# ConvFFN products in another order on VectorE and GpSimd, and the last normalisation and its stores regrouped

## The chip, the cores and the metric

The kernel runs on one core of a Trainium2 chip. The metric is the device time of one execution in microseconds (us), as the median of several runs. Five engines matter. TensorE (PE in the profile, PEld for its weight loads) multiplies matrices into PSUM. [...] ScalarE (ACT) evaluates activation functions and copies. SyncE (SP) issues most of the DMA transfers; ACT's queue issues a few. Each engine executes its own list of instructions strictly in the order of that list; an instruction that waits holds up all that stand behind it on its engine.

## What is computed

One inference step of a decoder with two layers, for 256 prompt tokens and 8 sample tokens that go through together as 264 columns. Each layer has a mixer (attention beside a gating or pooling branch) and then a ConvFFN; a last RMSNorm gives `y`. The change touches the ConvFFN and the last RMSNorm:

```python
def rmsnorm(x, g):
    xf = x.astype(jnp.float32)
    y = xf * lax.rsqrt(jnp.mean(xf * xf, axis=-1, keepdims=True) + EPS)
    return (y * g).astype(x.dtype)

def conv_ffn(x, prev, norm_g, w_gate, w_up, conv_w, conv_b, w_down):
    T = x.shape[1]
    h = rmsnorm(x, norm_g)
    g = h @ w_gate
    g_all = jnp.concatenate([prev, g], axis=1)
    gc = sum(conv_w[i] * g_all[:, i:i + T] for i in range(CONV_W)) + conv_b
    a = jax.nn.gelu(gc) * (h @ w_up)
    return x + a @ w_down, g_all[:, -(CONV_W - 1):]
```

The model width is 1024, the FFN width 2816; all values are float32.

## The kernel before

**Layout.** Activations lie transposed: 128 partitions of one feature tile, 264 tokens along the free axis. The model width is 8 tiles (`KD`), the FFN width 22 tiles (`NF`). Each weight matrix is cut into blocks of 128x128, laid out in HBM in the order in which TensorE uses them.

**Precision by halves.** Every operand is split in a rounded high half and the remainder, the low half. A weight tile of eight blocks is read as `raw` by DMA, copied to `wh` on ACT (L311) and its remainder `wl` formed on DVE (L312), both from rings of four buffers: tile t+4 can be split only when TensorE is done with tile t. Each block then takes three matmuls (L334 high x high, L335 high weight x low activation, L336 low weight x high activation). Activations are split the same way, by `halves` (L418 on ACT, L419 on DVE) or by `operand_tile` (L378 on ACT, L379 on DVE).

**The ConvFFN.** `ffn(l, ...)` runs the blocks of 22 gate tiles and 22 up tiles in turn, g0 u0 g1 u1 g2 u2 and so on, eight blocks each; only the first four output tiles are interleaved by half their depth. The results accumulate in four PSUM banks (tag `mm`), so a fifth output tile needs a bank that an earlier one has left. For the first five tiles (`JN`) the operand is `xg`, the residual times the norm's gain without the norm's scale R per token; R is multiplied in afterwards. For the later tiles the operand is `xn`, normalised beforehand: `normalise(m)` multiplies the residual by R on GpSimd (L533, result `xr`, two buffers) and splits the product (L378, L379). Eight of these are placed by hooks between the blocks 40 and 68 of the FFN; the sixth gate tile, g5, is the first that needs them.

A gate tile's evacuation `evac` for j < 5 multiplies the bank by R into the buffer G (L543, DVE), then forms the convolution in C from G: L546 on ACT, L547, L548, L549 on DVE, and L550 on ACT copies the last columns of G out. L551 on ACT is the gelu. C and G are the two halves of one tile `wk`. An up tile's evacuation multiplies C by R on GpSimd (L557), then the up tile's bank by C on DVE into A (L558), and splits A into `a_h` and `a_l`. A lies where G lay.

**The end.** After the second FFN's down projection each of the 8 residual tiles gets its square (L391), its gain (L580), and GpSimd adds the squares up (L403). `finish` sums over partitions on TensorE (L411) and makes R (L413, L414). Then each tile of X is multiplied by R, tiles 2 and 5 on GpSimd and six on DVE (L1000), and five stores of 1, 1, 2, 2 and 2 tiles send X to `y`, in turn from SP's and ACT's queue (L1002).

**What sets the order.** The program is written in one order, but a planner arranges each engine's list at compile time by its own timeline of the program (`schedule_with_timeline_sim=True`); what is marked `keep_in_program_order` stays in place. So the list of an engine can change where its instructions' dependences change.

## Time and profile before

| quantity | value |
|---|---|
| median of 3 runs | 633.56 us (632.65 to 635.03) |
| the profiled execution's own time | 632.96 us |
| span of its profile | 630.9 us |
| TensorE busy | 611.6 us, 97% of the span |
| VectorE busy | 413.2 us, 65% |
| ScalarE busy | 343.8 us, 54% |
| GpSimd busy | 82.5 us, 13% |
| granted TensorE clock, mean | 0.994 |

The span goes from the first to the last instruction; the time of the execution holds some 2.1 us more than it. A row of the timeline has the start, the duration in us, the engine, the line, the operation, the output and inputs with their shapes, and in brackets the engine's idle time before it and what ended it. Instructions of one engine overlap a little: 0.43 us of a VectorE product with a start 0.34 us behind the one before is usual. A matmul of 264 columns is listed with 0.28 us, but one starts every 0.12 us. The table of stretches gives, for each, the busy time and the count of each engine's instructions, the granted clock (1.00 is full speed), the mean busy share of the core's 16 DMA engines, and the GB/s that they moved.

### The profile page before, as it was taken

How to read it: one execution, taken by the hardware profiler on the slowest of the kernel's cores; microseconds unless marked ns; L12 is line 12 of the kernel's file. 1: busy time of each engine (PE TensorE's matmuls, PEld its weight loads, DVE VectorE, ACT ScalarE, POOL GpSimd, SP SyncE). 2: the span in 40 equal slices, each digit the busy share in tenths (PEclk: the TensorE clock that was granted, in tenths of full speed). 3: DMA queues.
4: the chain of work that ended last, by engine and by line, in shares of the span. 5: the costliest groups of instructions: out<-in, count | busy, mean ns of one | idle time of the engine just before them, and what ended most of it. 6: DMA issues, size and time to landing. Idle time of an engine off the chain costs nothing.

```text
span 630.9 us, 12406 instructions
## 1 busy us (share of the span) xinstructions
PE 611.6 (97%) x4956; PEld 583.2 (92%) x4956; DVE 413.2 (65%) x690; ACT 343.8 (54%) x608; POOL 82.5 (13%) x111
## 2 busy tenths in 40 slices
PE   7899999998999999999999999999899999999994
PEld 5887997998999999999998886999899999999994
DVE  6895674959966676655654674396996667664442
ACT  6448653667665555644442664366766555564441
POOL 3320132324000000010110000032400000001021
PEclk8999999999999999999999999999999999999998
DMA  7995673543555455795477679354355545554501
GB/s 271 324 414 223 238 262 72 182 156 132 200 201 180 161 195 198 228 382 202 179 189 300 230 117 112 129 172 169 128 200 200 179 166 191 201 165 177 200 1 70
DMA packets 40971, 121.42 MB, mean 192 GB/s; under 512 B 17490, under 2 KB 18642, under 8 KB 29522
## 3 DMA queue, kind: packets, MB, share of 16 engines
q1 hardware_dynamic: 40050, 119.15, 57.2%
q10 hardware_dynamic: 864, 1.49, 0.7%
q8 instruction: 39, 0.64, 0.4%
q14 instruction: 18, 0.15, 0.1%
HBM read 116.68 MB, written 3.94 MB: 191 GB/s over the span
## 4 chain that ended last, share of the span: by engine, by line
PE 90%; DVE 4%; ACT 2%; DMA 2%; issue 1%; POOL 1%; SPq 0%; DVEq 0%; ACTq 0%; POOLq 0%
PE mm L334 27%; PE mm L335 27%; PE mm L336 26%; DMA raw<-in_w 2%; DVE wl L312 1%; PE pv_l L470 1%; PE sc L456 1%; ACT wh L311 1%; PE Z L880 1%; PE Z L868 1%; PE pav L499 1%; DVE xn_l L379 1%; PE S L655 1%; PE S L654 1%; PE po_l L483 1%
## 5 line engine op out<-in xcount | busy, mean ns | idle before, releaser
L312 DVE TENSOR_TENSOR wl<-raw,wh 128x1024 fp32r<-128x1024 f32 x183 | 229.1, 1253 | 135.1 <-ACT wh L311 135.1
L311 ACT ACTIVATE wh<-raw 128x1024 fp32r<-128x1024 f32 x183 | 193.4, 1059 | 204.9 <-PE mm L335 187.6
L335 PE MATMUL mm<-xn_l,wh 128*128 128x264 f32 x544 | 154.4, 284 | 0.0
L336 PE MATMUL mm<-xn_h,wl 128*128 128x264 f32 x544 | 154.1, 283 | 0.0
L334 PE MATMUL mm<-xn_h,wh 128*128 128x264 f32 x544 | 153.9, 283 | 0.0
L334 PEld LDWEIGHTS mm<-xn_h,wh 128*128 128x128 f32 x544 | 102.3, 188 | 0.0
L335 PEld LDWEIGHTS mm<-xn_l,wh 128*128 128x128 f32 x544 | 102.3, 188 | 0.0
L336 PEld LDWEIGHTS mm<-xn_h,wl 128*128 128x128 f32 x544 | 102.2, 188 | 0.0
L335 PE MATMUL mm<-a_l,wh 128*128 128x264 f32 x352 | 99.9, 284 | 0.0
L336 PE MATMUL mm<-a_h,wl 128*128 128x264 f32 x352 | 99.7, 283 | 0.0
L334 PE MATMUL mm<-a_h,wh 128*128 128x264 f32 x352 | 99.5, 284 | 0.0
L335 PEld LDWEIGHTS mm<-a_l,wh 128*128 128x128 f32 x352 | 66.2, 188 | 0.0
L336 PEld LDWEIGHTS mm<-a_h,wl 128*128 128x128 f32 x352 | 66.2, 188 | 0.0
L334 PEld LDWEIGHTS mm<-a_h,wh 128*128 128x128 f32 x352 | 66.1, 188 | 0.0
L334 PE MATMUL mm<-xg_h,wh 128*128 128x264 f32 x160 | 46.9, 300 | 4.2 <-ACT wh L311 2.5
L334 PE MATMUL mm<-xg_f_h,wh 128*128 128x264 f32 x160 | 46.2, 289 | 4.5 <-DVE wk L558 4.3
L335 PE MATMUL mm<-xg_l,wh 128*128 128x264 f32 x160 | 45.6, 291 | 0.0
L336 PE MATMUL mm<-xg_f_h,wl 128*128 128x264 f32 x160 | 45.3, 283 | 0.0
L335 PE MATMUL mm<-xg_f_l,wh 128*128 128x264 f32 x160 | 45.3, 283 | 0.0
L336 PE MATMUL mm<-xg_h,wl 128*128 128x264 f32 x160 | 45.2, 294 | 0.1
L334 PE MATMUL mm<-xg_n_h,wh 128*128 128x264 f32 x128 | 37.9, 296 | 0.0
L335 PE MATMUL mm<-xg_n_l,wh 128*128 128x264 f32 x128 | 37.0, 289 | 0.0
(257 smaller groups left out, 1088.5 us busy)
## 6 DMA issues: line engine op xcount, KB each, us to landing
raw<-in_w SPq DMA_DIRECT2D x89, 1024.0 KB, 4.8
K<-in_kt SPq DMA_DIRECT2D x32, 256.0 KB, 6.2
V<-in_vp SPq DMA_DIRECT2D x32, 256.0 KB, 5.4
raw<-in_w SPq DMA_DIRECT2D x5, 512.0 KB, 5.1
CST<-in_cst SPq DMA_DIRECT2D x1, 560.0 KB, 4.7
XG<-in_x ACTq DMA_DIRECT2D x1, 528.0 KB, 7.7
out_k<-k SPq DMA_DIRECT2D x1, 528.0 KB, 8.7
out_v<-v SPq DMA_DIRECT2D x1, 528.0 KB, 3.0
```

The lines of the kernel that those rows point to most:

```text
L311: s.activation(h, src, AF.Copy)
L312: v.tensor_tensor(l, src, h.bitcast(F32), ALU.subtract)
L334: pe.matmul(o, h[:, c:c + P], xh, start=first, stop=False)
L335: pe.matmul(o, h[:, c:c + P], xl, start=False, stop=False)
L336: pe.matmul(o, l[:, c:c + P], xh, start=False, stop=left[m] == 0)
L379: j = v.scalar_tensor_tensor(l, src, gain, h.bitcast(F32), ALU.mult, ALU.subtract)
L456: pe.matmul(ps[32 * t:32 * t + 32, :PAST].rearrange("p (g k) -> p g k", g=NPG), qz[:, t, sq, :], kt[sq][:, :, t * P:(t + 1) * P], start=sq ...
L470: pe.matmul(pv[32 * j:32 * j + 32, :], pz[:, pg, sq, :], vtiles[sq][:, pg, :], start=pg == 0, stop=pg == NPG - 1)
L483: pe.matmul(po[:, t * NS:(t + 1) * NS], msk[:, gr, 2 * t:2 * t + 2, :].rearrange("p h d -> p (h d)"), cst("selS")[:, gr * NS:(gr + 1) * NS ...
L499: pe.matmul(o, vt[:, 0, h * HD:(h + 1) * HD], w[:, :SEQ], start=True, stop=False)
L654: pe.matmul(ps[:, 0:P], qh[:, 0:P], kh[:, 0:P], start=True, stop=False, skip_group_check=True)
L655: pe.matmul(ps[:, P:384], qh[:, P:SEQ], kh[:, 0:SEQ], start=False, stop=False, skip_group_check=True)
```

## The change

In the first five tiles of each FFN the up tile's evacuation multiplies the bank by R on VectorE into A, and GpSimd then multiplies A by C in place. Before, GpSimd multiplied C by R, and VectorE then the bank by C. The number of operations and their shapes stay. At the end, all eight tiles of X are multiplied on VectorE, in five instructions of 1, 2, 2, 2 and 1 tiles with R broadcast over the tiles, each followed by its store; and `y` in HBM has the tile as its outermost axis, so that a store writes rows of 264 floats where a store of two tiles had written rows of 528. The host's transposition of the output follows.

```diff
-YG = (2, 5)
-YD = ((0, 1), (1, 2), (2, 4), (4, 6), (6, 8))
-YQ = 1
+YD = ((0, 1), (1, 3), (3, 5), (5, 7), (7, 8))
...
-    ("y", (P, KD, T)), ("k0", (P, 4, T)), ("v0", (P, 4, T)), ("bvn", (P, 4, NS)),
+    ("y", (KD, P, T)), ("k0", (P, 4, T)), ("v0", (P, 4, T)), ("bvn", (P, 4, NS)),
...
                 C, A = wk[:, 0, :], wk[:, 1, :]
                 if j < JN:
-                    g.tensor_tensor(C, C, R, ALU.mult)
-                v.tensor_tensor(A, o, C, ALU.mult)
+                    v.tensor_tensor(A, o, R, ALU.mult)
+                    g.tensor_tensor(A, A, C, ALU.mult)
+                else:
+                    v.tensor_tensor(A, o, C, ALU.mult)
                 halves(*hl(act, j), A)
...
     R = nrm.finish()
-    for m in range(KD):
-        (g if m in YG else v).tensor_tensor(X[:, m, :], X[:, m, :], R, ALU.mult)
     for i, (m, e) in enumerate(YD):
-        (s if YQ and i % 2 else nc.sync).dma_start(a["y"][:, m:e, :], X[:, m:e, :])
+        x = X[:, m:e, :]
+        v.tensor_tensor(x, x, R.unsqueeze(1).to_broadcast([P, e - m, T]), ALU.mult)
+        (s if i % 2 else nc.sync).dma_start(a["y"][m:e].rearrange("m p t -> p m t"), x)
```

More of the change, by code (lines that the diff above doesn't have):

```diff
@@ L1047 @@
     o = {n: np.asarray(r.results[0]["out_" + n]) for n, _ in _OUTS}
-    y = o["y"].transpose(2, 1, 0).reshape(T, D)
+    y = o["y"].transpose(2, 0, 1).reshape(T, D)
     def kv(k, w):
```

## The prediction

> **What bounds the kernel now.** I read the page first. TensorE is busy for 97% of the span, so what is not matmul time can only be had where TensorE stands still, and at the end, where it has nothing left to do. The list of who waited for whom, taken over the start of each FFN, names one such wait, for L558, the line that the change rewrites. TensorE's timeline gives its places, here the last matmul before each stop and the first one behind it:

> ```profile
> 140.91 0.28 PE L336 MATMUL mm<-xg_f_h,wl 128*128 128x264 f32 x1
> 141.75 0.36 PE L334 MATMUL mm<-xg_f_h,wh 128*128 128x264 f32 x1 [0.56 <-DVE wk L558]
> 150.41 0.28 PE L336 MATMUL mm<-xg_f_h,wl 128*128 128x264 f32 x1
> 150.81 0.36 PE L334 MATMUL mm<-xg_f_h,wh 128*128 128x264 f32 x1
> 153.65 0.28 PE L336 MATMUL mm<-xg_f_h,wl 128*128 128x264 f32 x1
> 155.55 0.36 PE L334 MATMUL mm<-xg_f_h,wh 128*128 128x264 f32 x1 [1.62 <-DVE wk L558]
> ...
> 453.65 0.28 PE L336 MATMUL mm<-xg_f_h,wl 128*128 128x264 f32 x1
> 455.49 0.36 PE L334 MATMUL mm<-xg_f_h,wh 128*128 128x264 f32 x1 [1.55 <-DVE wk L558]
> ```

> With 0.12 us from start to start as the usual pace, TensorE loses 0.72, 0.28 and 1.78 us, together 2.8 us, and the second FFN shows the same stops (1.72 us in the longest). That is the ceiling of what the first part of the change can give: about 2.8 us a layer, 5.5 us in both.

> The two long stops have different causes, as the chain of waits (start, duration, what) shows:

> ```profile
> 139.17 0.42 ACT wk L551
> ...
> 139.66 1.49 POOL wk L557
> ...
> 141.17 0.44 DVE wk L558
> ...
> 145.90 1.76 DVE wl L312
> ...
> 148.93 0.47 DVE wk L548
> ...
> 150.66 0.76 DVE wk L548
> 151.42 1.70 DVE wl L312
> 153.12 0.93 DVE xn_l L379
> ...
> 154.99 0.43 DVE wk L558
> ```

> At 141 the up tile u0 holds its bank until the gelu (L551) and GpSimd's product (L557) are done. At 155 the chain has run along VectorE alone since 145.90: u1's product stood in a full list. VectorE's stretches say the same (us; then busy time and count of PE, PEld, DVE, ACT, POOL; clock, DMA share, GB/s):

> ```profile
> 150.00:156.00 6.00, 4.27 (x34) 3.90 (x33) 6.00 (x10) 3.84 (x8) 4.42 (x6) 1.00 0.29 120
> 156.00:162.00 6.00, 6.00 (x52) 6.00 (x51) 6.00 (x11) 3.80 (x8) 1.41 (x2) 1.00 0.47 164
> ```

> From 150 to 162 VectorE never rests. And what ends this crowded stretch is the next thing that TensorE waits for: the last low half `xn_l`, without which g5 cannot finish.

> ```profile
> 161.09 0.48 DVE L379 SCALAR_TENSOR_TENSOR xn_l<-xr,VEC,xn_h 128x264 fp32r<-128x264 f32 x1
> 161.08 0.40 PE L334 MATMUL mm<-xn_h,wh 128*128 128x264 f32 x2
> 161.32 0.29 PE L335 MATMUL mm<-xn_l,wh 128*128 128x264 f32 x1
> ```

> TensorE arrives there with almost no slack (a step of 0.24 in place of 0.12 us). So two paths meet at 161.3: TensorE's with 2.8 us of stops, and VectorE's with hardly any. Taking the stops away helps only as far as VectorE's list gets shorter too.

> **The change part by part. First, the products of the FFN.** Five VectorE products and five GpSimd products per layer are exchanged for as many of the same shapes (bank times SBUF operand, SBUF times SBUF), so busy time stays: 0.43 us each on VectorE, up to 1.49 us on GpSimd. What moves is when the bank is left. The new product needs the up tile, R, and the buffer A, which is G's: it must come behind L548 and L550, the last readers of G.

> ```profile
> 137.84 0.47 DVE L548 SCALAR_TENSOR_TENSOR wk<-wk,VEC 128x254 f32<-128x254 f32 x1
> 139.30 1.23 DVE L312 TENSOR_TENSOR wl<-raw,wh 128x1024 fp32r<-128x1024 f32 x1 [0.99 <-ACT wh L311]
> 141.17 0.43 DVE L558 TENSOR_TENSOR wk<-mm,wk 128x264 f32<-128x264 f32 x1 [0.64 <-POOL wk L557]
> 142.20 1.23 DVE L312 TENSOR_TENSOR wl<-raw,wh 128x1024 fp32r<-128x1024 f32 x1 [0.60 <-ACT wh L311]
> 143.34 0.43 DVE L419 TENSOR_TENSOR a_l<-wk,a_h 128x264 fp32r<-128x264 f32 x1
> 143.68 0.77 DVE L543 TENSOR_TENSOR wk<-mm,R_f 128x264 f32<-128x264 f32 x2
> 145.90 1.76 DVE L312 TENSOR_TENSOR wl<-raw,wh 128x1024 fp32r<-128x1024 f32 x1 [0.65 <-ACT wh L311]
> ```

> For u0 that is 138.31 us, in an idle stretch of 0.99 us; its bank is free at 138.7 and the stop of 0.72 goes. For u1, L548 runs at 148.93 (chain), its bank is free by 149.8, before g4 asks for one at 150.5 (the 0.28 us). u2's follows behind the L548 that the chain has at 150.66, free by 151.9, before u4 asks at 153.8 (the 1.78 us). All three stops lose their cause.

> What is late next is `xn_l`. Between 142.20 and 161.57 VectorE works 18.7 us and idles 0.65. The list does not shrink; it can only start earlier. The chain of the first tile loses a link: GpSimd ends at 141.15 as before, and ScalarE can form `a_h` at once (0.41 us) in place of a VectorE product first, so L419 and the two L543 behind it (0.35 us each by their starts) can run from 141.6, in the 0.60 us that VectorE idles before the split at 142.20. The 0.65 us before 145.90 goes too, since that split waits through ScalarE for u2, which ends 0.72 us earlier. That is 1.25 us; against it, u3's product, now behind `xn_l` at 161.50, moves ahead of it and costs 0.35 us. Net 0.9 us, with the 0.12 us at 161.32 about 1.0 us a layer, 2.0 us in both. Bounds: -0.35 us a layer if the planner keeps the idle places, +2.8 us if it puts two splits of `a` and g4's product (0.35 us each) and one weight split (1.2 us) behind the last `xn_l`. I take the value between, for the rows show no slack of 2.8 us in VectorE's list but show 1.25 us.

> New waits: ScalarE's `a_h` now waits for GpSimd, and behind it stand weight copies L311. If it is put ahead of the one that now starts at 141.11, that copy is late by 0.4 us; the `wl` from it, ready at 143.4, is first used from 150.81, so this costs nothing, and without that cover it would cost 0.4 us. GpSimd's new product waits for the gelu as the old one did, with the same L533 behind it. VectorE waits for GpSimd only through `a_l`, where it had waited in L558.

> **Second, the end.** Rows of VectorE, GpSimd and the queues:

> ```profile
> 624.50 1.86 DVE L1000 TENSOR_TENSOR XG<-XG,R_fin 128x264 f32<-128x264 f32 x2
> 624.20 1.87 POOL L1000 TENSOR_TENSOR XG<-XG,R_fin 128x264 f32<-128x264 f32 x2 [8.93 <-ACT R_fin L414]
> 626.97 0.42 DVE L1000 TENSOR_TENSOR XG<-XG,R_fin 128x264 f32<-128x264 f32 x1
> 624.61 0.34 SPq L1002 DMA_DIRECT2D out_y<-XG  x1
> L309 DVE TENSOR_TENSOR wl<-raw,wh 128x512 fp32r<-128x512 f32 x1 | 0.7, 692 | 0.0
> L757 DVE TENSOR_TENSOR bv<-bv,mu 128x1056 f32<-128x1056 f32 x1 | 1.3, 1259 | 0.2 <-ACT mu L756 0.2
> 625.00:625.50 0.50, 0.00 (x0) 0.00 (x0) 0.50 (x2) 0.00 (x0) 0.50 (x2) 1.00 0.05 17
> 625.50:626.00 0.50, 0.00 (x0) 0.00 (x0) 0.50 (x1) 0.00 (x0) 0.50 (x1) 1.00 0.73 254
> 628.00:628.50 0.50, 0.00 (x0) 0.00 (x0) 0.00 (x0) 0.00 (x0) 0.00 (x0) 0.50 1.00 380
> 629.00:629.50 0.50, 0.00 (x0) 0.00 (x0) 0.00 (x0) 0.00 (x0) 0.00 (x0) 0.50 0.84 325
> ```

> Beside GpSimd's two products, until 626.07, two of VectorE's take 1.86 us together, where two such products take 0.77 us (the L543 above). Without GpSimd, five instructions follow from 624.15: one of 264 columns, three of 528 (0.71 us by the 692 ns for 512; the broadcast adds nothing, by the 1259 ns for 1056), one of 264. With an overlap of 0.08 us they end at 624.58, 625.21, 625.84, 626.47 and 626.82; the last product ended at 627.39. So VectorE is 0.57 us sooner.

> The DMA engines are full from 628 (share 1.00) to about 629.4 us (0.84 of the last half microsecond), so the end is set by bytes as well. The first store, issued at 624.61, shows data from about 625.47 (the share of 0.05 in 625.0 to 625.5), 0.86 us later. The second then starts at 626.09 and the rest follows without a gap: seven tiles of 135 KB, 946 KB. Rows of 1056 bytes moved at 254 GB/s with a share of 0.73, so 348 GB/s at a full share; rows of 2112 bytes at 380. All rows of `y` are now of 1056 bytes: 2.72 us at 348, end at 628.8; 2.47 us at about 383, end at 628.6. Against 629.4 this saves 0.6 to 0.85 us; I take 0.7. The bounds: 0 if the doubled number of rows costs as much as the earlier start gives (285 GB/s), 0.9 at best. The store's issue is 0.33 us on either queue, and behind these issues nothing stands.

> [...]

> **The sum.** 632.96 us for the profiled execution (630.9 of it span), less 2.0 and 0.7: 630.3. The profiled execution lies 0.6 us under the median of the runs, 633.56; on that scale the forecast is 630.9 us.

> **The rivals.** (B) VectorE's list makes full room: all stops go, 5.5 + 0.7 = 6.2 us, 627.4. For it: four or five instructions ahead of the last `xn_l` are not needed by TensorE soon. Against: the full rows from 150 to 162. (C) The FFN gains nothing, because the order is kept and `xn_l` stays at 161.5, or because the product queues behind L548 so long that the bank comes no earlier; the end alone gives 0.7: 632.9. For it: TensorE meets `xn_l` without slack now. Against: 1.25 us of idle VectorE time whose cause the change removes. (D) Slower: with the first tiles' gate products done earlier, the planner puts the convolutions of g1 and g2 and the new products (0.40 + 0.08 + 0.40 + 0.35 us by their starts, 1.23 us a tile) ahead of the first `xn_l`. The eight `normalise` steps pass through two buffers, GpSimd to ScalarE to VectorE, so a first one that is 2.46 us late makes the last one as late: TensorE waits in g5 until about 163.8, 2.4 us a layer, less 0.7 at the end: 637.7. It decides from the point where the last `xn_l` ends later than 161.57. For it: this is the order in which the program is written. Against: now `xn_l` comes first there.

> **How the numbers follow.** Chances: my forecast (A) 0.47, with its own range 629.3 to 632.3; B 0.22, C 0.22, D 0.09. The range reaches from B less a little scatter to C with the runs' scatter of about 1 us: 627.0 to 634.0; D lies outside. A measurement of this kernel can tell about 0.5%, 3.2 us, from no change: faster means under 630.4. That takes B whole and two fifths of A: 0.41. Slower, over 636.7, takes D: 0.08. The rest, 0.51, is the same.

> **What would show it.** In the changed profile: no TensorE stop that ends with an up tile's product; that product right behind L548 of its tile; the stop of g5 at `xn_l` grown to 1 to 2 us, with the last `xn_l` about 1 us earlier. A g5 without a stop means B; an `xn_l` after 161.6 means D. At the end, VectorE's last product near 626.8 on the old scale, less what the FFNs gave, and DMA engines full from 626.1 for 2.5 to 2.7 us. The forecast is wrong if stops for banks remain, or if the stores take longer than 3.3 us from there.

## The result, and the profile after

| | before | changed |
|---|---|---|
| median of 7 runs | 633.56 us (632.65 to 635.03) | 629.24 us (628.98 to 631.10) |
| ratio, with its 95% interval | 1 | 0.9936 (0.9921 to 0.9952) |
| profiled execution, its own time | 632.96 us | 629.23 us |
| its span | 630.93 us | 626.98 us |
| mean granted clock | 0.994 | 0.997 |

The changed kernel is 0.64% faster, 4.3 us by the medians and 3.95 us by the two spans. To see where it came from, the span is cut at four landmarks that both timelines have: ScalarE's copy of the 27th weight tile split there, which lies a little ahead of the first FFN, and the last residual sum of the first FFN, of the second mixer and of the second FFN (L575). Timelines of ScalarE (ACT in the rows) and VectorE (DVE), before and then changed (start, duration, engine, line, operation, tiles and shapes, and in brackets the idle time before it with what ended it):

```profile
114.50 1.06 ACT L311 ACTIVATE wh<-raw 128x1024 fp32r<-128x1024 f32 x1 [0.40 <-PE mm L335]
321.63 0.43 DVE L575 TENSOR_TENSOR XG<-XG,mm 128x264 f32<-128x264 f32 x1 [0.67 <-PE mm L336]
426.30 0.42 DVE L575 TENSOR_TENSOR XG<-XG,mm 128x264 f32<-128x264 f32 x1
621.44 0.43 DVE L575 TENSOR_TENSOR XG<-XG,mm 128x264 f32<-128x264 f32 x1 [7.59 <-PE mm L336]
```

```profile
114.15 1.06 ACT L309 ACTIVATE wh<-raw 128x1024 fp32r<-128x1024 f32 x1 [0.40 <-PE mm L333]
319.84 0.43 DVE L575 TENSOR_TENSOR XG<-XG,mm 128x264 f32<-128x264 f32 x1 [0.68 <-PE mm L334]
424.52 0.42 DVE L575 TENSOR_TENSOR XG<-XG,mm 128x264 f32<-128x264 f32 x1
617.99 0.43 DVE L575 TENSOR_TENSOR XG<-XG,mm 128x264 f32<-128x264 f32 x1 [7.59 <-PE mm L334]
```

Differences of these starts give the stretches (the last one runs to the end of the span): start 114.50 and 114.15, first FFN 207.13 and 205.69, second mixer 104.67 and 104.68, second FFN 195.14 and 193.47, end 9.49 and 8.99 us. So the first FFN gave 1.43 us, the second 1.66, the end 0.50 (differences from unrounded starts), the mixer nothing. The 0.35 us of the start belong to an execution, not to the change: that stretch comes out up to 2.3 us later in other kernels that share its code (last section).

In the changed kernel (line numbers two lower: matmuls L332 to L334, `xn_l` L377, the gate tile's last convolution step L546; the new products are L555 on VectorE and L556 on GpSimd, POOL in the rows) the list of who waited for whom at the start of the first FFN has one row for TensorE's matmuls, and TensorE's timeline shows its place (the second here) and a shorter stop ahead of it:

```profile
PE mm L333 <- DVE xn_l L377: 0.7, 1, 0.7
```

```profile
157.36 0.28 PE L332 MATMUL mm<-xn_h,wh 128*128 128x264 f32 x1
157.75 0.39 PE L333 MATMUL mm<-xn_l,wh 128*128 128x264 f32 x1
...
159.45 0.28 PE L333 MATMUL mm<-xn_l,wh 128*128 128x264 f32 x1
160.46 0.39 PE L333 MATMUL mm<-xn_l,wh 128*128 128x264 f32 x1 [0.73 <-DVE xn_l L377]
```

No stop ends with an up tile's product any more. The 0.72, 0.28 and 1.78 us of before are gone, and two stops for the last two `xn_l` have come: 0.27 and 0.89 us over the usual step. 2.78 us less 1.16 us is 1.62 us; the first FFN became 1.43 us shorter, so this account holds to 0.2 us. Counted matmul by matmul, the changed kernel is 1.65 us ahead from there to the end of the up tiles and loses the 0.2 us evenly over the down projection, without a stop; the second FFN (1.66 us) shows no such loss. VectorE's timeline shows what the stops now wait for:

```profile
137.49 0.48 DVE L546 SCALAR_TENSOR_TENSOR wk<-wk,VEC 128x254 f32<-128x254 f32 x1
138.00 0.43 DVE L555 TENSOR_TENSOR wk<-mm,R_f 128x264 f32<-128x264 f32 x1
...
141.28 0.43 DVE L417 TENSOR_TENSOR a_l<-wk,a_h 128x264 fp32r<-128x264 f32 x1 [1.11 <-ACT a_h L416]
141.63 0.77 DVE L541 TENSOR_TENSOR wk<-mm,R_f 128x264 f32<-128x264 f32 x2
...
148.61 0.42 DVE L555 TENSOR_TENSOR wk<-mm,R_f 128x264 f32<-128x264 f32 x1
...
150.07 0.42 DVE L555 TENSOR_TENSOR wk<-mm,R_f 128x264 f32<-128x264 f32 x1
...
157.96 0.42 DVE L555 TENSOR_TENSOR wk<-mm,R_f 128x264 f32<-128x264 f32 x1
158.30 1.21 DVE L310 TENSOR_TENSOR wl<-raw,wh 128x1024 fp32r<-128x1024 f32 x1
159.43 0.97 DVE L377 SCALAR_TENSOR_TENSOR xn_l<-xr,VEC,xn_h 128x264 fp32r<-128x264 f32 x1
```

The first up tile's product stands right behind L546 of its tile, the next two are done by 149.0 and 150.5. The split `a_l` (L417) runs at 141.28 where it ran at 143.34. From there on VectorE has no idle time at all, and the last `xn_l` ends at 160.40: 46.25 us behind the landmark, 47.07 before (161.57 less 114.50).

At the end, VectorE's five products and the stretches in which the stores move (columns: stretch, length, then busy time and count of PE, PEld, DVE, ACT, POOL; clock, DMA share, GB/s):

```profile
620.71 2.63 DVE L1001 TENSOR_TENSOR XG<-XG,R_fin 128x264 f32<-128x264 f32 x5 [2.29 <-ACT R_fin L412]
```

```profile
623.00:623.50 0.50, 0.00 (x0) 0.00 (x0) 0.34 (x1) 0.00 (x0) 0.00 (x0) 0.99 1.03 338
623.50:624.00 0.50, 0.00 (x0) 0.00 (x0) 0.00 (x0) 0.00 (x0) 0.00 (x0) 0.50 1.02 344
624.00:624.50 0.50, 0.00 (x0) 0.00 (x0) 0.00 (x0) 0.00 (x0) 0.00 (x0) 0.50 1.02 361
625.00:625.50 0.50, 0.00 (x0) 0.00 (x0) 0.00 (x0) 0.00 (x0) 0.00 (x0) 0.50 0.86 300
```

The products take 2.63 us where they took some 3.2 (624.15 to 627.39). The DMA engines are full from 623.0 to about 625.4, at 338 to 361 GB/s.

### The profile page after: what moved, and what is told of

It is laid out like the page before. It is cut to its first block, busy times and chain, and to the rows that moved or that the text cites. A ratio compares the mean times of both kernels' runs of the same rounds, so it can differ in the third digit from the quotient of the medians.

```text
span 627.0 us, 12404 instructions
## 1 busy us (share of the span) xinstructions
PE 610.4 (97%) x4956; PEld 581.9 (93%) x4956; DVE 414.2 (66%) x689; ACT 344.8 (55%) x608; POOL 84.0 (13%) x109
## 4 chain that ended last, share of the span: by engine, by line
PE 88%; DVE 6%; ACT 2%; issue 2%; DMA 1%; POOL 1%; SPq 0%; DVEq 0%; ACTq 0%; POOLq 0%
PE mm L332 26%; PE mm L333 26%; PE mm L334 26%; DVE wl L310 2%; DVE xn_l L377 1%; PE pv_l L468 1%; DMA raw<-in_w 1%; PE sc L454 1%; PE Z L880 1%; PE Z L868 1%; ACT wh L309 1%; PE pav L497 1%; DVE wk L545 1%; PE S L655 1%; PE S L654 1%
## 5 line engine op out<-in xcount | busy, mean ns | idle before, releaser
L309 ACT ACTIVATE wh<-raw 128x1024 fp32r<-128x1024 f32 x183 | 193.7, 1059 | 198.6 <-PE mm L333 184.9
L332 PE MATMUL mm<-xn_h,wh 128*128 128x264 f32 x544 | 153.9, 283 | 0.0
L334 PE MATMUL mm<-xn_h,wl 128*128 128x264 f32 x544 | 153.8, 283 | 0.0
L332 PEld LDWEIGHTS mm<-xn_h,wh 128*128 128x128 f32 x544 | 102.3, 188 | 0.0
L334 PEld LDWEIGHTS mm<-xn_h,wl 128*128 128x128 f32 x544 | 102.1, 188 | 0.0
L332 PE MATMUL mm<-a_h,wh 128*128 128x264 f32 x352 | 99.6, 284 | 0.0
L334 PE MATMUL mm<-a_h,wl 128*128 128x264 f32 x352 | 99.5, 283 | 0.0
L334 PEld LDWEIGHTS mm<-a_h,wl 128*128 128x128 f32 x352 | 66.2, 188 | 0.0
L332 PEld LDWEIGHTS mm<-a_h,wh 128*128 128x128 f32 x352 | 66.1, 188 | 0.0
L332 PE MATMUL mm<-xg_h,wh 128*128 128x264 f32 x160 | 46.4, 297 | 3.6 <-ACT wh L309 1.4
L334 PE MATMUL mm<-xg_h,wl 128*128 128x264 f32 x160 | 44.5, 290 | 1.3 <-DVE wl L310 1.3
L332 PE MATMUL mm<-xg_f_h,wh 128*128 128x264 f32 x160 | 45.7, 286 | 0.0
L334 PE MATMUL mm<-xg_f_h,wl 128*128 128x264 f32 x160 | 45.4, 283 | 0.0
L333 PE MATMUL mm<-xg_f_l,wh 128*128 128x264 f32 x160 | 45.3, 283 | 0.0
L332 PE MATMUL mm<-xg_n_h,wh 128*128 128x264 f32 x128 | 37.9, 296 | 0.0
```

Source lines behind the costliest of these rows:

```text
L309: s.activation(h, src, AF.Copy)
L332: pe.matmul(o, h[:, c:c + P], xh, start=first, stop=False)
L333: pe.matmul(o, h[:, c:c + P], xl, start=False, stop=False)
L334: pe.matmul(o, l[:, c:c + P], xh, start=False, stop=left[m] == 0)
```

## The experiments

Twelve kernels ran. The first table has their times beside the kernel before on the same chip; the second cuts their profiles into the stretches above, as differences from before, with TensorE's stops (over 0.15 us beyond the usual step) added up over each FFN stretch. The stretches are the finer instrument: the second mixer's reproduces to 0.01 us in all kernels but two (six tiles -0.20, fifth bank -0.08).

| kernel | runs | median us | before us | ratio (95%) |
|---|---|---|---|---|
| FFN products alone | 6 | 631.11 | 633.21 | 0.9963 (0.9945 to 0.9981) |
| end alone | 10 | 632.38 | 633.21 | 0.9989 (0.9975 to 1.0003) |
| changed, `y` in long rows | 6 | 629.84 | 633.21 | 0.9946 (0.9928 to 0.9965) |
| changed, A times C on VectorE | 5 | 628.58 | 633.21 | 0.9931 (0.9909 to 0.9954) |
| changed, six tiles | 4 | 628.15 | 632.81 | 0.9918 (0.9887 to 0.9949) |
| changed, four `xr` buffers | 6 | 629.50 | 632.81 | 0.9943 (0.9924 to 0.9963) |
| changed, `normalise` earlier | 4 | 629.02 | 632.81 | 0.9922 (0.9897 to 0.9948) |
| before, fifth bank | 10 | 631.01 | 632.81 | 0.9965 (0.9946 to 0.9983) |
| before, own banks for up tiles | 4 | 639.96 | 633.29 | 1.0109 (1.0088 to 1.0130) |
| all three, new products | 4 | 629.02 | 633.29 | 0.9932 (0.9914 to 0.9949) |
| all three, old products | 4 | 629.53 | 633.29 | 0.9936 (0.9914 to 0.9958) |
| all three, A times C on VectorE | 10 | 633.13 | 633.29 | 0.9996 (0.9976 to 1.0016) |

| profile | start | FFN 1 | FFN 2 | end | stops FFN 1, 2 |
|---|---|---|---|---|---|
| before (us) | 114.50 | 207.13 | 195.14 | 9.49 | 2.97, 2.90 |
| changed | -0.35 | -1.43 | -1.66 | -0.50 | 1.35, 1.30 |
| FFN products alone | +1.31 | -1.43 | -1.68 | +0.32 | as changed |
| end alone | -0.10 | +0.01 | +0.01 | -0.50 | as before |
| long rows | +2.34 | -1.44 | -1.66 | -0.85 | as changed |
| A times C on VectorE | +0.14 | -2.06 | -2.02 | -0.49 | 0.99, 0.98 |
| six tiles | +0.05 | -2.13 | -2.06 | -0.14 | 0.49, 0.66 |
| four `xr` buffers | -0.31 | -1.55 | -1.79 | -0.05 | 1.39, 1.35 |
| `normalise` earlier | +1.48 | -1.42 | -1.33 | -0.50 | 1.16, 1.15 |
| fifth bank | +4.11 | -2.84 | -3.19 | 0.00 | 0.98, 0.99 |
| own banks | +0.04 | +3.35 | +3.37 | 0.00 | 4.83, 4.82 |
| all three, new products | +1.57 | -1.57 | -1.49 | -0.40 | 1.59, 1.61 |
| all three, old products | +1.94 | -1.81 | -1.71 | -0.85 | 1.36, 1.38 |
| all three, A times C on VectorE | +0.63 | +0.50 | +0.58 | -0.85 | 2.13, 2.14 |

**The two parts alone.** The kernel before with only the five lines of the FFN products changed, and with only the end changed.

> The kernel before with the FFN products alone in the new order; end and stores as before. My theory (the banks of the up tiles are free earlier, and what is then late is the last low half xn_l on VectorE): the profile of the whole change shows 1.65 us gained in each FFN, so this kernel gains 3.3 us, span 627.6, time about 630.2 us. The longest wait of TensorE is about 0.9 us for xn_l in the sixth gate tile. Rival (the gain comes mostly from the end of the kernel): gain under 1 us, over 632.5 us.

> The kernel before with the end alone changed: products on VectorE by pairs, stores with the tile outermost; the FFN as before. My theory (the end is worth what its profile shows between the last residual sum and the end of the span, 0.5 us): span about 630.4, time 633.0 us. The rival above: over 3 us gained, about 630 us. The TensorE stops before the up tiles' banks stay, 0.72 and 1.78 us.

The FFN products alone give -1.43 and -1.68 us in the FFN stretches, what the whole change gives there; the end alone gives -0.50 us and leaves the FFNs as they were. The parts add up and don't touch each other. (The end stretch has scatter of its own: 9.49 us in three profiles with the old end and 9.81 in this one; with the new end 8.99 to 9.01 in four, 9.36 and 9.45 in two; with long rows 8.64 in three and 9.09 in one. The lower values are compared.) In whole times the first is 2.1 us (ratio below 1 with its interval), where 3.3 were expected: its profile has the gain in the FFNs, but a start 1.31 us and an end 0.32 us longer. The second is 0.8 us, with an interval that holds 1.

**Long rows of `y`.** The changed kernel, with `y` laid out as before, so that a store of two tiles writes rows of 2112 bytes:

```diff
-        (...).dma_start(a["y"][m:e].rearrange("m p t -> p m t"), x)
+        (...).dma_start(a["y"][:, m:e, :], x)
```

> The changed kernel with y in the layout of before, so that a store of two tiles writes rows of 2112 bytes; the products by pairs on VectorE stay. If the length of the rows sets the pace of the stores, the stretch with busy DMA engines at the end is shorter by 0.2 to 0.25 us (380 against 350 GB/s for 946 KB) and the kernel takes about 629.0 us. Rival (rows of 1056 bytes cost nothing, the stores wait for their issue): no difference in the end, 629.2 us, the same GB/s at a full share.

The end takes 8.64 us: the short rows cost 0.35 us. Its stores, in the same columns:

```profile
626.00:626.50 0.50, 0.00 (x0) 0.00 (x0) 0.02 (x1) 0.00 (x0) 0.00 (x0) 0.50 1.06 401
```

401 GB/s at a share of 1.06, against 338 to 361 at 1.02 to 1.03. Its whole time doesn't show the gain (0.9946 beside 0.9936); its profiled execution began 2.34 us late.

**A times C on VectorE.** The changed kernel with both products on VectorE, so that its list has five instructions more per layer:

```diff
-                    g.tensor_tensor(A, A, C, ALU.mult)
+                    v.tensor_tensor(A, A, C, ALU.mult)
```

> The changed kernel with the second product, A times C, on VectorE in place of GpSimd: five more VectorE instructions of 0.43 us a layer. If VectorE's full list sets the time of the last xn_l (my theory), the three of them that stand ahead of it make it 1.05 us later, the stop in g5 grows by that much, and the kernel loses about 2 us: 631.3 us. Rival (the latency of the chain through GpSimd sets it): the chain is 1.1 us shorter, the stop shrinks, and the kernel takes 628 us or less.

If the number of VectorE's instructions set the last `xn_l`, this would be slower. The FFN stretches became 0.63 and 0.36 us shorter still, so the expectation failed. The stop for `xn_l` is gone: the last one ends 0.67 us sooner, and the matmul that waits for it stands five places later in TensorE's list. Two short stops for a bank have come. The first waits for a gate product L541 that stands behind a weight split and `a_l` again (143.83 us, where the changed kernel has it at 141.63); the second comes while u1's product, which frees a bank at 148.61 us in the changed kernel, stands at 152.41. TensorE's and VectorE's timelines:

```profile
144.40 0.36 PE L332 MATMUL mm<-xg_f_h,wh 128*128 128x264 f32 x1 [0.17 <-DVE wk L541]
...
150.74 0.36 PE L332 MATMUL mm<-xg_f_h,wh 128*128 128x264 f32 x1 [0.30 <-DVE wk L541]
```

```profile
159.75 0.48 DVE L377 SCALAR_TENSOR_TENSOR xn_l<-xr,VEC,xn_h 128x264 fp32r<-128x264 f32 x1
```

The last `xn_l` takes 0.48 us here and 0.97 in the changed kernel, where GpSimd's new product runs beside it:

```profile
158.60 1.51 POOL L556 TENSOR_TENSOR wk<-wk 128x264 f32<-128x264 f32 x1 [1.19 <-DVE wk L555]
```

Both lose: the same GpSimd shape takes 0.75 us in other rows (`xr` at 150.39 in the changed kernel). The stretch of 148 to 162 us, in which VectorE never rests in either kernel, has the effect as a whole, changed and then this one:

```profile
148.00:162.00 14.00, 13.17 (x106) 12.75 (x105) 14.00 (x24) 9.53 (x18) 7.40 (x7) 1.00 0.43 151
```

```profile
148.00:162.00 14.00, 13.70 (x114) 13.52 (x113) 14.00 (x29) 9.74 (x19) 3.31 (x4) 1.00 0.43 151
```

With GpSimd busy for 3.31 us in place of 7.40, VectorE gets through 29 instructions in place of 24: two of the five products that it takes over, and more of the convolution. The six `xn_l` of the stretch take 3.4 us in place of 4.8, which is more than the 0.8 us of the two products. How the rows of the changed kernel lie beside each other: GpSimd's product starts at 158.60 beside the weight split of 158.30 to 159.51 and ends at 160.11; the `xn_l` that starts beside it at 159.43 ends at 160.40. That split takes 1.21 us, as one does with GpSimd idle (160.80), so here it was GpSimd's product and the `xn_l` that took longer; a split at 150.41, with GpSimd busy all through, takes 1.82 us. The products that read a bank keep their 0.42 us beside GpSimd (149.73 and 150.07; GpSimd is busy from 149.47 to 151.14). What makes the difference no run shows.

**Six tiles, four buffers, earlier normalisation.** Three ways to take the stop for `xn_l` away from the changed kernel: a sixth tile with `xg` (`JN` 5 to 6), four buffers of its own for `xr` in place of two, and `normalise` placed 16 blocks earlier (`NA` 4 to 2).

> The changed kernel with six tiles instead of five that take R afterwards, so that xn is first needed by the seventh gate tile, 5.8 us later. My theory (what TensorE waits for now is the lateness of the last xn_l in g5, 1.2 us a layer): the stop in g5 goes, and nothing takes its place; 2.4 us less, about 626.9 us. Rival (VectorE and ScalarE, with one more G and product for each layer, pass the lateness on to the weight splits): a stop for wl or for a bank of about the same size appears, 629 us or more.

> The changed kernel with four buffers for xr, GpSimd's product that xn is split from, in place of two that it shares. Theory 1 (round trips through two buffers over GpSimd, ScalarE and VectorE hold the xn_l back): the last xn_l comes at least 1 us earlier, the stop in g5 is gone, 626.9 us. Theory 2 (VectorE's time sets it, including what it loses beside GpSimd): the last xn_l moves by less than 0.3 us, 629.2 us.

> The changed kernel with the eight normalise steps placed 16 blocks (5.8 us) earlier in the program. Theory 1 (the steps start too late): the first and the last xn_l come over 1 us earlier and the stop in g5 goes, 626.9 us. Theory 2 (VectorE's time): the first xn_l comes earlier, but what it pushes back returns as a wait for a bank of an early tile; the same within 0.5 us, 629.2 us.

The sixth tile takes the FFNs to -2.13 and -2.06 us, with stops of 0.49 and 0.66 us left (0.20 of them stand in every kernel), so 1.1 us of the expected 2.4 came. With four buffers the last `xn_l` starts 39.9 us behind the landmark, 5.4 us sooner than the 45.3 of the changed kernel, and the stop for it is gone, but the stretches are only 0.12 and 0.13 us better: the buffers did hold the `xn_l` back, as Theory 1 had it, and the time that it gave did not follow. A stop for an up tile's bank is back: the product that lets go of it starts at 150.05, where the changed kernel had it at 148.61, with more `xn_l` done ahead of it. TensorE's timeline:

```profile
150.62 0.36 PE L332 MATMUL mm<-xg_f_h,wh 128*128 128x264 f32 x1 [1.03 <-DVE wk L555]
```

The earlier normalisation moves the last `xn_l` by 2.4 us and gets a stop of 0.65 us for a gate tile's bank, and one of 0.31 us, in its place; nothing is gained.

**Banks without the new products.** First the kernel before with five banks for output tiles in place of four (`MMB`), which leaves the mixers three others in place of four. Then the kernel before with the first five up tiles in banks of the mixers' pool, which an FFN leaves empty:

```diff
-                ps[m] = psm.tile([P, 512], F32, tag="mm", name=f"mm{i}")
+                ps[m] = at(f"sp{i}") if m in spare else psm.tile(...)
```

> The kernel before, its products in the old order, with five PSUM banks for the matmuls in place of four (three are left for the rest). My theory of the first gain (the up tile's bank is held too long): the stops of 0.72, 0.28 and 1.78 us in each FFN go without any change of the products; the last xn_l stays within 0.3 us of its place, so TensorE waits for it about 1.5 us, and an FFN is about 1.3 us shorter. Rival (the gain came from VectorE's earlier start, not from the bank): an FFN is shorter by less than 0.4 us. The mixers have a bank less and may get slower, so the FFN is read alone, from the landmarks.

> Kernel before, but the first five up tiles of each FFN accumulate in banks of the pool that the mixers use and that the FFN leaves empty, so no gate tile waits for an up tile's bank; products, their engines and the end are those of before. Theory (what the change did in the FFN is only to let go of the bank early): the stops at 141.75, 150.81 and 155.55 us are gone, TensorE comes some 2.8 us sooner to the matmuls that need the last xn_l and, with 1.2 to 1.3 us of slack there, stops for 1.2 to 1.6 us at it; from the split of weight tile 27 to the last residual sum 205.4 to 205.9 us in the first FFN (207.1 before, 205.7 with the change), 193.2 to 193.8 in the second, the stretch from there to the span's end as before (9.5 us); time about 630.2 us. Rival (the gain comes from VectorE's shorter chain of the first tile, not from the banks): these two stretches stay within 0.5 us of 207.1 and 195.1, because xn_l stays where it was and TensorE waits there for all that it has gained; time about 632.5 us.

With the fifth bank, and the old products, the three stops are gone and a stop of 0.79 us for an `xn_l` is left: 2.0 us less of stops in the first FFN, 1.9 in the second. (The stretches shrink by 2.84 and 3.19 us, but the landmarks moved by 4 and 8 matmuls there, 0.5 and 1.0 us.) So an early bank by itself does what the new products do. The last `xn_l` ends 46.85 us behind the landmark (47.07 before), and no stop waits for it; the 0.79 us are for the one ahead of it. The matmul that needs the last one stands 12 places later in TensorE's list than in the kernel before. So the gain did not need an earlier `xn_l` here: what a free bank is worth depends also on where the planner puts that matmul. The first mixer lost in turn: the start grew by 4.11 us, of which other executions without this edit show up to 2.3, so the price of the missing bank is not well known; 3.4 us of it ran at half the clock (92.78 to 96.19 us), as no other profile shows in that stage.

With banks of their own the three stops are gone too, and yet the kernel is 6.7 us slower, against both expectations. A new stop stands 57 us behind the landmark. The lists that lead to it, ScalarE's, VectorE's and TensorE's:

```profile
171.72 0.18 ACT L550 ACTIVATE cvo<-mm 128x10 f32<-128x10 f32 x1 [1.05 <-DVE wk L548]
```

```profile
166.94 2.36 DVE L312 TENSOR_TENSOR wl<-raw,wh 128x1024 fp32r<-128x1024 f32 x2 [0.52 <-ACT wh L311]
169.22 0.48 DVE L547 SCALAR_TENSOR_TENSOR wk<-mm,VEC,wk 128x255 f32<-128x255 f32 x1
169.61 0.16 DVE L549 TENSOR_TENSOR wk<-wk,C 128x8 f32<-128x8 f32 x1
169.68 1.22 DVE L312 TENSOR_TENSOR wl<-raw,wh 128x1024 fp32r<-128x1024 f32 x1
170.82 0.48 DVE L547 SCALAR_TENSOR_TENSOR wk<-mm,VEC,wk 128x255 f32<-128x255 f32 x1
171.21 0.47 DVE L548 SCALAR_TENSOR_TENSOR wk<-mm,VEC,wk 128x254 f32<-128x254 f32 x1
```

```profile
168.02 0.29 PE L336 MATMUL mm<-xn_h,wl 128*128 128x264 f32 x1
171.95 0.39 PE L334 MATMUL mm<-xn_h,wh 128*128 128x264 f32 x1 [3.65 <-ACT cvo L550]
```

From the sixth tile on a gate tile's bank is read by its whole convolution, up to the copy L550. Here three weight splits (2.36 and 1.22 us) stand before and among the convolution steps in VectorE's list, L550 comes at 171.72, and TensorE stands still for 3.81 us. Of the 3.35 us that the first FFN lost, 1.86 are stops, and 1.5 the half clock that follows (last section). The weight ring is part of it: TensorE came to this place sooner and so let go of its weight buffers sooner, and the splits that they allow went ahead of the convolution. That last link is read from the order of the rows; no run tried it by itself.

**All three together.** The changed kernel with own banks for the up tiles, four `xr` buffers and long rows; the same with the old products; and the same with both products on VectorE.

> The changed kernel with the spare banks for the first five up tiles, four buffers instead of two for the products of X and R that GpSimd makes for xn, and y in its old layout (rows of two tiles). Theory: no bank stop and no stop for xn_l is left, so the two FFN stretches are 2.8 and 3.2 us shorter than before (204.3 and 192.0 us), and the end takes 8.7 us instead of 9.5: time about 626.5 us. Rival (more buffers make GpSimd run beside VectorE earlier and slow it, as the run with four buffers alone showed with a bank stop of 1.2 us; or the splits of A come so late that g5's matmuls wait): stretches of 205.5 and 193.4, time about 629 us.

> As the kernel before it in this list (spare banks, four buffers, y in its old layout, the new end), but with the old order of the first five tiles' products: GpSimd multiplies C by R, VectorE the bank by C. Theory: with banks and buffers to spare the order of the products no longer matters; stretches within 0.4 us of the run with the new order, about 204.3 and 192.0 us; time about 626.5 us. Rival (the new order also takes a link out of the first tile's chain, and that is worth something by itself): 0.4 to 1 us longer in each FFN, time 627.3 to 628.5 us.

> As the run with spare banks, four buffers, y in its old layout, the new end and the new order of products, but the product of A and C is on VectorE too. Theory (GpSimd's products beside VectorE cost VectorE more than one product more does): the last xn_l comes no later, no stop of TensorE over 0.4 us, stretches 204.0 to 204.4 and 191.8 to 192.2 us; time 626.2 to 626.6 us. Rival (VectorE's five products more fill its list): a stop for xn_l or for an up tile's half of 0.5 to 1.5 us, time 627 to 629 us.

Neither stop of the changed kernel is left in any of them, and none reaches the 626.5 us that I expected. Each has the gate bank's stop instead, 1.39, 1.17 and 1.93 us. The old products do as well as the new ones here (-1.81 and -1.71 against -1.57 and -1.49 us), so with banks to spare their order is worth nothing. The third kernel is no faster than before. Its last `xn_l` comes no later than in the first (39.3 us behind the landmark in both), but its stop is 0.5 us longer and, in the profiled execution, followed by a stretch at half the clock (last section), about 1.5 us in each FFN.

No kernel of these is shown by its whole time to beat the changed one: the best, with six tiles, has 0.9918 (0.9887 to 0.9949) beside 0.9936 (0.9921 to 0.9952). By the FFN stretches some do, six tiles and A times C on VectorE most, by 1.1 and 1.0 us in both layers together.

## Why the prediction was right, point by point

- **The stops lose their cause.** Right. All three are gone, the products stand where the prediction put them for the first up tile, and the fifth bank, which frees nothing but banks, does the same.
- **What is late next is `xn_l`.** Right, and the size of the stop too: 1.16 us, where 1 to 2 were forecast. The last `xn_l` ends 0.82 us sooner, where the net was 0.9. Its parts came out otherwise: it starts 1.30 us sooner (45.29 against 46.59 behind the landmark), the product of u3 did move ahead of it, and it takes 0.97 us in place of 0.48 beside GpSimd's new product. The prediction had called busy time unchanged and left that out.
- **TensorE's slack there, 0.12 us.** Wrong, and this is the mis-sized term of the FFN. The row it came from, 161.08, has the count x2: two matmuls in one row, so 0.24 us is two usual steps and no wait at all. Nor can the matmul at 161.32 be the one that needs the last `xn_l`, which ends at 161.57. Blocks run L334, L335, L336, but at 161.08 two L334 follow one another: the planner put the L335 of the first of them off, behind the L334 at 162.67. TensorE's timeline of the kernel before:

```profile
162.67 0.28 PE L334 MATMUL mm<-xn_h,wh 128*128 128x264 f32 x1
162.79 0.29 PE L335 MATMUL mm<-xn_l,wh 128*128 128x264 f32 x1
162.91 0.28 PE L336 MATMUL mm<-xn_h,wl 128*128 128x264 f32 x1
163.04 0.28 PE L335 MATMUL mm<-xn_l,wh 128*128 128x264 f32 x1
```

  By the semaphores of the trace the one at 162.79 waits for the last `xn_l`, so the slack was 1.22 us. In the changed kernel that matmul stands two places sooner in the list (0.24 us), TensorE comes there 2.63 us sooner, and `xn_l` ends 0.82 us sooner: 2.63 and 0.24 less 0.82 less 1.22 is a wait of 0.83 us, and 0.89 was measured. So the term of 1.0 us a layer becomes 0.82 for `xn_l` and 0.98 for the slack, 1.8 us, of which 0.16 is lost again: the wait was 0.06 us longer than that, and the step behind it (160.46 to 160.68) 0.10 longer than the usual 0.12. The stretches show 1.43 and 1.66.
- **The end, 0.7 us.** Measured 0.50. VectorE's gain was right (2.63 us from start to end, where 2.67 was worked out). The choice between the two paces was not: 0.6 us belonged to 348 GB/s and 0.85 to 383, and I took a value between. The rows of the changed kernel show 338 to 361, and the run with long rows shows what the other pace gives, 0.85 us. So the short rows cost 0.35 us of 2.7.
- **The sum.** 2.0 and 0.7 were forecast, 3.09 and 0.50 measured, which is 3.6 us; the remaining 0.35 of the spans' 3.95 is in the start and owes nothing to the change. The misses of the two terms have opposite signs, so a small part of the agreement is luck. The median, 629.24 us, lies 1.7 us under the forecast of 630.9 us: inside the range, but 0.06 us under the forecast's own narrower one, 629.3 to 632.3. It is also under the 630.4 us that the prediction took as the bound of faster, an outcome to which it gave 0.41.
- **The rivals.** All stops gone (B) did not come, because `xn_l` stops TensorE. No gain in the FFN (C) fell with the FFN products alone. The late `xn_l` (D) did not come: the planner put the products of u1 and u2 ahead of several `xn_l`, but the list had gained more by its earlier start. Its idea, that something on VectorE is pushed in front of what TensorE needs next, is what made the kernel with own banks slower, at another place.

## What to carry to other kernels

A stop that ends with a bank's release is worth only the distance to the next thing that is late, so work out that distance from both sides: how much sooner the next operand comes, and how much slack TensorE has there, by finding the matmul that reads that operand, counting matmuls and reading the x count of merged rows. Where lists are laid out by a planner, more buffers can make a kernel slower: in the kernel with own banks, other work stood ahead of the step that releases the next bank. An element-wise operation moved to GpSimd is not always free for VectorE: beside GpSimd's product an `xn_l` took 0.97 us here in place of 0.48, while a product that reads a bank kept its 0.42 us beside GpSimd.

## What the runs showed of the hardware

**A stop of under 2 us can cost the clock.** Stretches around three stops (columns as above; the clock is the third figure from the end): of 1.93 us in the kernel with all three and both products on VectorE, of 1.78 us in the kernel before, and of 3.84 us in the second FFN of the kernel with own banks:

```profile
167.74:171.15 3.41, 1.64 (x14) 1.45 (x13) 3.41 (x10) 2.10 (x6) 0.00 (x0) 1.00 0.59 250
171.15:174.56 3.41, 3.41 (x18) 3.41 (x17) 1.27 (x4) 1.32 (x3) 0.00 (x0) 0.50 0.72 250
```

```profile
152.40:155.82 3.42, 1.80 (x15) 1.62 (x14) 3.42 (x7) 1.64 (x3) 2.27 (x2) 1.00 0.00 0
```

```profile
469.86:473.27 3.41, 1.72 (x15) 1.51 (x13) 3.03 (x5) 3.41 (x6) 0.00 (x0) 1.00 0.15 62
473.27:476.68 3.41, 1.43 (x11) 1.43 (x12) 3.41 (x7) 1.24 (x4) 0.00 (x0) 1.00 0.82 303
476.68:480.09 3.41, 3.41 (x18) 3.41 (x17) 1.46 (x4) 1.71 (x5) 0.00 (x0) 0.50 0.82 276
```

**The start differs between executions by more than this change gives in an FFN.** In the same stretch of the start, before and in the kernel with all three and the old products:

```profile
24.00:28.00 4.00, 3.46 (x28) 3.49 (x29) 2.69 (x7) 2.39 (x3) 1.36 (x2) 1.00 0.95 356
```

```profile
24.00:28.00 4.00, 3.59 (x17) 3.62 (x18) 1.05 (x3) 1.54 (x2) 1.22 (x2) 0.57 0.95 365
```

In the one TensorE does 28 rows of matmuls at full clock, in the other 17 at 0.57; this one's start is 1.94 us longer. But the kernel before has a stretch at half the clock of the same length, from 12.46 to 15.87 us, and in others the start is longer with none at all (the earlier normalisation: +1.48 us). So the low clock by itself does not explain the difference, and I did not find what does. It is why stretches between landmarks told these kernels apart where whole times could not.
